# Six of a recurrent branch's eight output gates as seven-product pairs, computed behind the output projection

## The chip, the core and the metric

One core of a Trainium2 chip runs the whole layer. The metric is device time in microseconds (us); the time before is the median of three runs. TensorE multiplies, VectorE and ScalarE do elementwise work and empty TensorE's banks (PSUM), GpSimd (POOL) does elementwise work on SBUF, and SyncE (SP) issues the DMAs. In the profile PE is TensorE's matmul and PEld its weight load.

## The reference, cut to what matters

The layer is macaron FFN, mixer, macaron FFN, each modulated by a per-sample vector. In the mixer:

```
proj = h @ w_in
q, k, v, xr, yr, g_att, g_rec = jnp.split(proj, idx, axis=-1)
att = chunked_attention(q, k, v, rel_bias) @ w_att_o
xr = causal_depthwise_conv(xr, conv_w, conv_b)
rec = (rg_lru(xr, ...) * jax.nn.gelu(yr)) @ w_rec_o
merged = jax.nn.sigmoid(g_att) * att + jax.nn.sigmoid(g_rec) * rec
return merged @ w_out
```

Sequence, model width and recurrent width are 1024, all in float32. The stage of this case computes the gate g_rec and the projection by w_rec_o, and writes their product to DRAM (`part`), where a later stage fetches it.

## The kernel before, in words

A float32 matrix is cut into a high and a low part (`split`: ScalarE casts to the high part, VectorE or GpSimd subtracts for the low one), and one product of 128x128 weights with 512 columns takes three matmuls: high x high, high x low, low x high (`mm3`, L492 to L494). `proj` computes one block of 128 output channels: two halves of the sequence, eight chunks of depth, 48 matmuls.

The stage `rec_out_phase` has eight gate blocks ("gr", input `hh`, `hl`) and eight output blocks ("ro", input `rec_h`, `rec_l`), all by `proj`. They alternate: gate 0, gate 1, output 0, gate 2, output 1, and so on. ScalarE applies a tanh to a gate (L1289), VectorE multiplies it into the output (L1301), SP writes it to `part`. `Weights` loads weights two blocks ahead (`prep_cols`, `prep`); the float32 tile has the tag "raw" (three buffers), the parts "wh" and "wl" (four each).

Beside this runs `bg`: four modulation vectors, each of eight loads of 512 KB into the same "raw" buffers (`ada_acc`, SP), eight products on VectorE (L207, L209), and then eight narrow matmuls (`pc`, L223; the first two vectors) or four matmuls from a split accumulator (`pg`, L311 and L312; the two gates). A call `bg(4)` records four steps; it is called before and after each output block. Temporary tiles `tu` have three buffers, `t4` 22.

The scheduler of the language orders this stage: it places the recorded instructions of each engine in a fixed order, by its own rules. In a `tc.manual_schedule` region the engines named keep the order of the code; SP's DMAs are placed by the scheduler. Each engine executes its list from top to bottom. The FFN phases already use a seven-product scheme (`mix`, `product`, `block`): two products of halves of weights and input are combined so that seven of 12 matmuls replace eight, at the price of sums of weights and inputs.

Before this stage runs the recurrence (`lru_phase.rest`), behind it attention (`att_phase`), whose first matmuls (L1359) are the q and k projections.

Of the kernel before, what the change touches and what calls it, by code (L numbers as in the profile page):

```python
# [50 lines left out]
def kernel(  # L51
# [49 lines left out]
    def bank(name):  # L101
        return ps[0].tile([P, 512], F32, tag="ps", bufs=nbank[0], name=nm(name))
# [1003 lines left out]
    C_Q, C_K, C_V, C_XR, C_YR, C_GA, C_GR = 0, 512, 1024, 1536, 2560, 3584, 4608  # L1106
# [38 lines left out]
    def lru_phase(hh, hl, tail):  # L1145
# [125 lines left out]

        return SimpleNamespace(fetch=wts.fetch, head=head, rest=rest)

    def rec_specs():
        specs = {}
        for n in range(KB + 1):
            if n < KB:
                specs["gr", n] = partial(prep_cols, w_in, C_GR + n * P)
            if n > 0:
                specs["ro", n - 1] = partial(prep_cols, w_rec_o[0], (n - 1) * P)  # L1280
        for n in ("q", "k"):
            specs[n, 0] = partial(prep_cols, w_in, (C_Q if n == "q" else C_K))
        return specs

    def rec_out_phase(hh, hl, rec_h, rec_l, wts, part):
        def gate(n):
            tg = tu("tg")
            for sh, pj in enumerate(proj(wts["gr", n], hh, hl)):
                nc.scalar.activation(tg[:, sh * 512 : (sh + 1) * 512], pj, AF.Tanh, scale=0.5)  # L1289
            return tg  # L1290

        nxt = gate(0)
        for n in range(KB):
            tg = nxt
            if n + 1 < KB:
                nxt = gate(n + 1)
            bg(4)
            pr = proj(wts["ro", n], rec_h, rec_l)
            for sh in range(2):
                sl = slice(sh * 512, (sh + 1) * 512)  # L1300
                nc.vector.scalar_tensor_tensor(tg[:, sl], tg[:, sl], 1.0, pr[sh], op0=ALU.add, op1=ALU.mult)  # L1301
            nc.sync.dma_start(part[n * P : (n + 1) * P, :], tg)
            bg(4)
        bg_flush()

    def att_phase(hh, hl, wts0, tg_dram, n_ga):
        att_h, att_l = [], []
# [618 lines left out]
    with tc.tile_pool(name="psA", bufs=1, space=PSUM) as psA, tc.tile_pool(name="tmpA", bufs=1) as tmpA:  # L1926
        ps[0], tmp[0] = psA, tmpA
        with tc.manual_schedule(engines=ALL_ENGINES):
            hh, hl = new_h()
            f1 = ffn(0, ffn1_w_gu, ffn1_w_down, hh, hl, x, out if upto == 1 else x1)  # L1930
            startup(f1, hh, hl)
        bgq.extend([ada_gate(0, 0.5), ada_cols(3), ada_cols(4)])
        if upto == 1:
            f1.run(None, None, 3)
            return
        nxt = new_h()
        lru_run = lru_phase(*nxt, rec_specs())
# [6 lines left out]
        rec_out_phase(hh, hl, rec_h, rec_l, wts, part)  # L1944
    n_ga = sum(GATES)
    att_h, att_l = att_phase(hh, hl, wts, tg_dram, n_ga)
    with tc.tile_pool(name="psB", bufs=1, space=PSUM) as psB, tc.tile_pool(name="tmpC", bufs=1) as tmpC:
# [4 lines left out]
        nxt = new_h()  # L1952
# [45 lines left out]
```

## Time and profile before

| what | value |
|---|---|
| median of three runs | 2185.45 us (2184.38 to 2185.84) |
| the profiled execution's own time | 2184.91 us |
| its span | 2183.1 us |
| granted TensorE clock, mean | 0.997 |

How to read it: the page gives each engine's busy time; the time windows give it for stretches, with the granted clock and the DMA share; the groups join instructions of one line, operation and shape, with count, mean ns of one and the idle time ahead of them with what ended it; the timeline shows single instructions (start, duration, engine, line, out<-in, idle time before and who ended it). A matmul of TensorE is shown with its full length, and the next starts before it ends.

### The profile page before, as it was taken

Reading aid. Unit: us, or ns where it says so; the run is one execution under the profiler, and the core shown is the slowest. Engines: PE = TensorE matmul, PEld = TensorE weight load, DVE = VectorE, ACT = ScalarE, POOL = GpSimd, SP = SyncE. Lnnn points to the kernel's source line nnn. Section 1 sums busy time; section 2 is a strip of 40 time slices with the busy share of each in tenths; the row PEclk is TensorE's granted clock in tenths of the full one; section 3 lists DMA queues with packets and bytes.
Section 4 is the critical chain, followed back from the end, with each engine's and each line's share of the span. In section 5 each row is a group of like instructions: output and inputs, shape, how many; then the busy total and the mean of one; then the engine's idle time right before and its main releaser. Section 6 shows DMA issues by size and latency. Waiting matters only on the chain.

```text
span 2183.1 us, 26770 instructions
## 1 busy us (share of the span) xinstructions
PE 2142.9 (98%) x9973; PEld 1778.6 (81%) x9973; DVE 1311.2 (60%) x1699; ACT 1015.7 (47%) x1572; POOL 699.3 (32%) x514
## 2 busy tenths in 40 slices
PE   7999999999999999999999999999999999999998
PEld 5878788888878888888898988888888888888877
DVE  7676675567467777654236666555686564544466
ACT  5443333334447787611147777436443333334443
POOL 1468895421104011000121120002168883522102
PEclk9999999999999999999999999999999999999999
DMA  9357674468575111276311011464357663347365
GB/s 326 90 177 261 226 260 154 138 219 317 189 248 189 48 51 42 75 240 211 132 49 61 26 56 55 147 196 164 111 197 260 238 220 111 113 152 274 127 230 184
DMA packets 261498, 358.36 MB, mean 164 GB/s; under 512 B 16720, under 2 KB 170488, under 8 KB 261368
## 3 DMA queue, kind: packets, MB, share of 16 engines
q1 hardware_dynamic: 248448, 310.43, 43.0%
q10 hardware_dynamic: 12920, 46.23, 5.5%
q8 instruction: 78, 1.28, 0.2%
q14 instruction: 52, 0.43, 0.1%
HBM read 265.37 MB, written 94.37 MB: 165 GB/s over the span
## 4 chain that ended last, share of the span: by engine, by line
PE 79%; DVE 6%; ACT 4%; DMA 2%; issue 1%; POOL 1%; SPq 0%; POOLq 0%; DVEq 0%; ACTq 0%
PE px L1008 8%; PE pv L1008 7%; PE pj L494 6%; PE pj L492 6%; PE pj L493 6%; PE psX L747 6%; PE psX L748 6%; PE psX L749 6%; PE pj L1359 5%; PE psZ L747 3%; PE psZ L749 3%; PE psZ L748 3%; PE pv L1406 2%; DMA rawd<-downs 1%; PE psY L749 1%; PE psY L747 1%
## 5 line engine op out<-in xcount | busy, mean ns | idle before, releaser
L149 ACT CAST dh<-rawd 128x1024 fp32r<-128x1024 f32 x154 | 161.1, 1053 | 204.2 <-PE px L1008 60.1
L150 DVE TENSOR_TENSOR dh<-rawd,dh 128x1024 fp32r<-128x1024 f32 x130 | 162.3, 1253 | 153.2 <-ACT dh L149 148.6
L738 DVE TENSOR_TENSOR wm<-raw,wm 128x512 fp32r<-128x512 f32 x152 | 162.5, 1073 | 152.4 <-ACT wm L737 149.5
L492 PE MATMUL pj<-hh,wh 128*128 128x512 f32 x562 | 220.8, 393 | 0.0
L493 PE MATMUL pj<-hl,wh 128*128 128x512 f32 x562 | 219.2, 390 | 0.8 <-DVE hl L355 0.8
L494 PE MATMUL pj<-hh,wl 128*128 128x512 f32 x562 | 219.4, 390 | 0.3 <-DVE wl L150 0.2
L1008 PE MATMUL px<-dh,dh 128*128 128x512 f32 x608 | 187.5, 390 | 1.2 <-DVE dh L150 1.2
L344 POOL TENSOR_SCALAR rstd<-rstd 128x1 f32<-128x1 f32 x47 | 29.9, 636 | 424.4 <-ACT junk L343 423.0
L1008 PE MATMUL pv<-dh,dh 128*128 128x512 f32 x528 | 163.2, 391 | 2.4 <-DVE dh L150 2.4
L149 ACT CAST wh<-raw 128x1024 fp32r<-128x1024 f32 (+1 forms) x84 | 84.7, 1011 | 145.3 <-DMA raw<-in_w_in_dram 41.7
L150 POOL TENSOR_TENSOR wl<-raw,wh 128x1024 fp32r<-128x1024 f32 x20 | 48.3, 2421 | 294.6 <-ACT wh L149 249.9
L946 POOL TENSOR_TENSOR act<-act,act 128x512 f32<-128x512 f32 x54 | 87.2, 1614 | 160.7 <-DMA act<-act 115.9
L1008 PE MATMUL px<-dh 128*128 128x512 f32 x352 | 137.4, 390 | 0.0
L1008 PEld LDWEIGHTS px<-dh,dh 128*128 128x128 f32 x608 | 114.0, 188 | 25.4 <-DVE dh L150 2.0
L494 PEld LDWEIGHTS pj<-hh,wl 128*128 128x128 f32 x562 | 105.5, 188 | 22.9 <-DVE wl L150 1.2
L493 PEld LDWEIGHTS pj<-hl,wh 128*128 128x128 f32 x562 | 105.6, 188 | 22.8 <-DVE hl L355 1.4
L492 PEld LDWEIGHTS pj<-hh,wh 128*128 128x128 f32 x562 | 105.7, 188 | 21.3 <-DVE a L527 0.3
L150 DVE TENSOR_TENSOR wl<-raw,wh 128x1024 fp32r<-128x1024 f32 (+1 forms) x64 | 73.7, 1155 | 78.0 <-ACT wh L149 77.8
L1008 PEld LDWEIGHTS pv<-dh,dh 128*128 128x128 f32 x528 | 98.8, 188 | 24.4 <-DVE dh L150 4.1
L747 PE MATMUL psX<-hh,wm 128*128 128x512 f32 x296 | 115.6, 390 | 2.1 <-ACT mixes L770 2.1
L747 PE MATMUL psX<-hs,wm 128*128 128x512 f32 x296 | 115.8, 391 | 1.3 <-ACT mixes L763 1.1
L749 PE MATMUL psX<-hs,wm 128*128 128x512 f32 x296 | 115.3, 389 | 0.0
(335 smaller groups left out, 5717.8 us busy)
## 6 DMA issues: line engine op xcount, KB each, us to landing
rawa<-in_w_ada_dram SPq DMA_DIRECT2D x56, 512.0 KB, 4.7
raw<-in_ffn_w_gu_dram SPq DMA_DIRECT2D x47, 512.0 KB, 5.5
rawd<-acts SPq DMA_DIRECT2D x88, 256.0 KB, 3.8
rawd<-downs SPq DMA_DIRECT2D x88, 256.0 KB, 4.1
raw<-in_w_in_dram SPq DMA_DIRECT2D x44, 512.0 KB, 3.7
act<-act SPq DMA_DIRECT2D x37, 512.0 KB, 5.0
acts<-act ACTq DMA_DIRECT2D x36, 512.0 KB, 4.0
sr<-in_ffn_w_gu_dram SPq DMA_DIRECT2D x35, 512.0 KB, 6.0
```

The costliest lines, as they stand in the source:

```text
L149: nc.scalar.copy(hi, raw)
L150: (eng or nc.vector).tensor_tensor(lo, raw, hi.bitcast(F32), op=ALU.subtract)
L492: nc.tensor.matmul(dst, wh[:, kk, :], xhk[:, sl], start=first, stop=False)
L493: nc.tensor.matmul(dst, wh[:, kk, :], xlk[:, sl], start=False, stop=False)
L494: nc.tensor.matmul(dst, wl[:, kk, :], xhk[:, sl], start=False, stop=last)
L738: nc.vector.tensor_tensor(t[:, 1], src, t[:, 0].bitcast(F32), op=ALU.subtract)
L747: nc.tensor.matmul(dst, t[:, 0, kk, :], xh, start=first and kk == 0, stop=False, skip_group_check=True)
L748: nc.tensor.matmul(dst, t[:, 0, kk, :], xl, start=False, stop=False, skip_group_check=True)
L749: nc.tensor.matmul(dst, t[:, 1, kk, :], xh, start=False, stop=last and kk == 3, skip_group_check=True)
L946: nc.gpsimd.tensor_tensor(o, p, q, op=op)
L1008: nc.tensor.matmul(dst, a_[:, 0, tk], w_[:, 1, :], start=first and n == 0, stop=last and n == 2, skip_group_check=True,)
L1359: nc.tensor.matmul(d, a[:, k, :], b[k][:, sl], start=k == 0 and i == 0, stop=k == KB - 1 and i == 2)
```

## The change

Gate blocks 0 and 4 stay plain and come first. Then the eight output blocks follow each other, in the order 0, 4, 1, 5, 2, 6, 3, 7. For 0 and 4 gate and output are multiplied as before. The other six outputs are copied to SBUF by ScalarE (`pr`) and written to DRAM (`rec_raw`). `bg` is called with 8 steps before and 4 after each output block. The sums of the input that the pairs need are recorded here too, six of them (`sum_of`, `combine`: three operations on VectorE, a cast on ScalarE, a low part on VectorE).

Then, in the order of the code (`manual_schedule`), the gates (1, 5), (2, 6), (3, 7) are computed as pairs: the weights of the two blocks are mixed by VectorE (`mix`) to seven sets, each cut into parts; `product` does 12 matmuls of one set with halves or sums of the input. Products 1, 2, 5 and 3 run pair by pair, then 6 over the pairs, then 7, then 4. `chain[j]` is a bank (`grX`) into which products 1, 6, 7 and 4 of a pair add up, `b2` (`grY`) takes product 2, `b3` (`grZ`) products 5 and 3; copies and additions between them form the gates `T`. `close` fetches the raw output and multiplies. The weights of q and k are loaded from here (`qk_w`).

```diff
+    GR_PLAIN = (0, 4)
+    GR_PAIRS = ((1, 5), (2, 6), (3, 7))
+    RO_ORDER = (0, 4, 1, 5, 2, 6, 3, 7)
...
+        def combine(i, kk, plus, minus):
+            t = tv("hsum")
+            vec(t, *plus, ALU.add)
+            for m in minus:
+                vec(t, t, m)
+            hs[i, kk] = s = t4("hs", F32R, (P, 2, 512))
+            nc.scalar.copy(s[:, 0], t)
+            vec(s[:, 1], t, s[:, 0].bitcast(F32))
...
+        def mix(j, i):
+            g, u = raws[j]
+            a, b, c, e = g[:, :4], g[:, 4:], u[:, :4], u[:, 4:]
+            if i == 5:
+                vec(c, a, c)
+                vec(a, a, c)
+                vec(a, a, e, ALU.add)
+            if i == 3:
+                vec(a, e, c)
+                vec(b, b, a)
+            src = {1: a, 2: b, 5: a, 3: b, 6: a, 7: c, 4: e}[i]
...
+            nc.scalar.copy(t[:, 0], src)
+            vec(t[:, 1], src, t[:, 0].bitcast(F32))
...
-        nxt = gate(0)
-        for n in range(KB):
-            tg = nxt
-            if n + 1 < KB:
-                nxt = gate(n + 1)
-            bg(4)
+        tgs = {n: gate(n) for n in GR_PLAIN}
+        early_sums = [(5, kk) for kk in range(4)] + [(6, 0), (6, 1)]
+        for at, n in enumerate(RO_ORDER):
             pr = proj(wts["ro", n], rec_h, rec_l)
+            bg(8)
...
+                sum_of(*early_sums[at - 2])
             bg(4)
         bg_flush()
...
+            for j, (n, m) in enumerate(GR_PAIRS):
+                T[n], T[m] = t4("tg"), t4("tg")
+                chain[j], b2 = bank("grX"), trbank("grY")
+                product(j, 1, chain[j], True)
+                nc.scalar.copy(T[n][:, h1], chain[j])
+                if j < 2:
+                    mix(j + 1, 1)
+                product(j, 2, b2, True)
+                vec(T[n][:, h1], T[n][:, h1], b2, ALU.add)
+                nc.scalar.activation(T[n][:, h1], T[n][:, h1], AF.Tanh, scale=0.5)
+                if j < 2:
+                    mix(j + 1, 2)
+                    some(1)
+                else:
+                    mix(0, 6)
+                b3[j] = bank("grZ")
+                product(j, 5, b3[j], True)
+                nc.scalar.copy(T[m][:, h2], b3[j])
...
+                product(j, 3, b3[j], False)
...
+            for j, (n, m) in enumerate(GR_PAIRS):
+                product(j, 6, chain[j], False)
+                nc.scalar.copy(T[n][:, h2], chain[j])
+                vec(T[n][:, h2], T[n][:, h2], b3[j], ALU.add)
+                nc.scalar.activation(T[n][:, h2], T[n][:, h2], AF.Tanh, scale=0.5)
+                mix(j, 7)
+                some(1)
...
+            for j, (n, m) in enumerate(GR_PAIRS):
+                product(j, 4, chain[j], False)
+                close(n)
+                nc.scalar.activation(T[m][:, h1], chain[j], AF.Tanh, scale=0.5)
```

What becomes of the order. First TensorE at the first modulation vector. Before, the column matmuls `pc` of its accumulator stand between a gate block (`pj_7290`, input `hh`) and an output block (`pj_7361`, input `rh`):

```order
L493 MATMUL pj_7290<-hl_958,wh_7143 128x512
L494 MATMUL pj_7290<-hh_950,wl_7144 128x512
L223 MATMUL pc_7342<-ones_r,acc_7199 128x1 x8
L492 MATMUL pj_7361<-rh_5918,wh_7213 128x512
L493 MATMUL pj_7361<-rl_5919,wh_7213 128x512
```

After, they stand inside the second output block (`pj_7303`, `pj_7304`, block 4), behind 15 of its 48 matmuls:

```order
L493 MATMUL pj_7303<-rl_6289,wh_7144 128x512
L494 MATMUL pj_7303<-rh_6288,wl_7145 128x512
L223 MATMUL pc_7284<-ones_r,acc_7256 128x1 x8
L492 MATMUL pj_7304<-rh_6288,wh_7144 128x512
L493 MATMUL pj_7304<-rl_6289,wh_7144 128x512
```

They moved forward by 33 matmuls of this block and by the gate block that stood ahead of them.

Second, the fourth vector. ScalarE casts the two halves of its accumulator (`acch`), TensorE multiplies them (`pg`). Before, on ScalarE, the last output weights (`wh_8019`, `wh_8077`) stand ahead of the second half's cast:

```order
L149 CAST acch_7937<-acc_7791 128x512
L149 CAST wh_7943<-raw_7941 128x1024
L149 CAST wh_8019<-raw_8017 128x1024
L149 CAST wh_8077<-raw_8075 128x1024
L149 CAST acch_8004<-acc_7791 128x512
```

After, the weights of the last two output blocks (`wh_7622`, `wh_7689`) stand behind both casts and behind a copy of an earlier output (`pr_7676`):

```order
L149 CAST acch_7589<-acc_7505 128x512
L149 CAST acch_7608<-acc_7505 128x512
L1393 COPY pr_7676<-pj_7626 128x512
L149 CAST wh_7622<-raw_7620 128x1024
L1393 COPY pr_7676<-pj_7627 128x512
L149 CAST wh_7689<-raw_7687 128x1024
```

What moved is the weight of the seventh output block, from ahead of the vector's second half to behind it.

Third, ScalarE in the pair stage, which has no counterpart before: there it held for each gate two tanh, beside casts of weights and of the vectors' halves:

```order
L1289 ACTIVATE tg_7716<-pj_7724 128x512
L149 CAST wh_7871<-raw_7869 128x1024
L1289 ACTIVATE tg_7868<-pj_7875 128x512
L1289 ACTIVATE tg_7868<-pj_7876 128x512
L149 CAST acch_7937<-acc_7791 128x512
```

After, for the second pair (`tg_8002`, `tg_8003`; `wm` are parts of mixed weights, `hs` parts of input sums), between the copies of `grX` and `grZ`:

```order
L1417 COPY tg_8002<-grX_8004 128x512
L1361 CAST wm_8019<-raw_7903 128x512
L1422 ACTIVATE tg_8002<-tg_8002 128x512
L1361 CAST wm_8036<-raw_7903 128x512
L1307 CAST hs_8043<-hsum_8039 128x512
L1430 COPY tg_8003<-grZ_8046 128x512
L1361 CAST wm_8063<-raw_7903 128x512
```

The copy of `grZ`, on which product 3 of this pair waits, is behind the cast of an input sum and behind the tanh. VectorE's list between the same two points:

```order
L1294 TENSOR_TENSOR tg_8002<-tg_8002,grY_8005 128x512
L1294 TENSOR_TENSOR wm_8036<-raw_7903,wm_8036 128x512
L1294 TENSOR_TENSOR hsum_8039<-hh_948,hl_956 128x512
L1294 TENSOR_TENSOR hsum_8039<-hsum_8039,hh_944 128x512
L1294 TENSOR_TENSOR hsum_8039<-hsum_8039,hl_952 128x512
L1294 TENSOR_TENSOR hs_8043<-hsum_8039,hs_8043 128x512
L1294 TENSOR_TENSOR sr_7904<-raw_7903,sr_7904 128x512
```

Each `wm` and `hs` row subtracts a part that ScalarE's row of the same name has just cast. L1294 is `vec`, the helper of all these operations.

More of the change, by code (lines that the diff above doesn't have):

```diff
@@ L1283, in rec_specs, with vec, f32 @@
         return specs
     def rec_out_phase(hh, hl, rec_h, rec_l, wts, part):
+        h1, h2 = slice(0, 512), slice(512, 1024)
+        rec_raw = dpool.tile([D, S], F32, name="rec_raw")
+        qk_w = Weights({
+            (n, 0): partial(prep_cols, w_in, (C_Q if n == "q" else C_K)) for n in ("q", "k")
+        })
+        def vec(out, p, q, op=ALU.subtract):
+            nc.vector.tensor_tensor(out, p, q, op=op)
+        def f32(t, sl):
+            return t[:, sl].bitcast(F32)
+        hs = {}
@@ new lines, in combine, with both, halves @@
+        def combine(i, kk, plus, minus):
[6 more added lines that the diff above has]
+            vec(s[:, 1], t, s[:, 0].bitcast(F32))
+        def both(k, sl):
+            return f32(hh[k], sl), f32(hl[k], sl)
+        def halves(i, kk):
+            t = hs[i, kk]
+            return t[:, 0].bitcast(F32), t[:, 1].bitcast(F32)
@@ new lines, in rec_out_phase, with load @@
+        raws, mixed = {}, {}
+        def load(j):
+            n, m = GR_PAIRS[j]
+            g = wpool.tile([P, KB, P], F32, tag="raw", bufs=3, name=nm("raw"))
+            u = t4("sr", F32, (P, KB, P))
+            for t, c in ((g, n), (u, m)):
+                c0 = C_GR + c * P
+                nc.sync.dma_start(t, w_in[:, c0 : c0 + P].rearrange("(k p) n -> p k n", p=P))
+            raws[j] = g, u
+        turn = [0]
+        def mix(j, i):
+            g, u = raws[j]
+            a, b, c, e = g[:, :4], g[:, 4:], u[:, :4], u[:, 4:]
+            if i == 5:
+                vec(c, a, c)
[5 more added lines that the diff above has]
+            src = {1: a, 2: b, 5: a, 3: b, 6: a, 7: c, 4: e}[i]
+            tag = ("wh", "wl")[turn[0] % 2]
+            turn[0] += 1
+            t = wpool.tile([P, 2, 4, P], F32R, tag=tag, bufs=4, name=nm("wm"))
+            nc.scalar.copy(t[:, 0], src)
+            vec(t[:, 1], src, t[:, 0].bitcast(F32))
+            mixed[j, i] = t
@@ L1286, in gate, with product @@
+        def product(j, i, dst, first):
+            t = mixed.pop((j, i))
+            for kk in range(4):
+                xh, xl = moving(i, kk)
+                nc.tensor.matmul(dst, t[:, 0, kk, :], xh, start=first and kk == 0, stop=False, skip_group_check=True)
+                nc.tensor.matmul(dst, t[:, 0, kk, :], xl, start=False, stop=False, skip_group_check=True)
+                nc.tensor.matmul(dst, t[:, 1, kk, :], xh, start=False, stop=kk == 3, skip_group_check=True)
         def gate(n):
@@ new lines, in rec_out_phase @@
+        early_sums = [(5, kk) for kk in range(4)] + [(6, 0), (6, 1)]
+        for at, n in enumerate(RO_ORDER):
+            pr = proj(wts["ro", n], rec_h, rec_l)
+            bg(8)
+            if n in tgs:
+                tg = tgs.pop(n)
+                for sh in range(2):
+                    sl = slice(sh * 512, (sh + 1) * 512)
+                    nc.vector.scalar_tensor_tensor(tg[:, sl], tg[:, sl], 1.0, pr[sh], op0=ALU.add, op1=ALU.mult)
+                nc.sync.dma_start(part[n * P : (n + 1) * P, :], tg)
+            else:
+                t = tu("pr")
+                for sh in range(2):
+                    nc.scalar.copy(t[:, sh * 512 : (sh + 1) * 512], pr[sh])
+                nc.sync.dma_start(rec_raw[n * P : (n + 1) * P, :], t)
+                sum_of(*early_sums[at - 2])
@@ L1303, in rec_out_phase, with some, close @@
             bg(4)
         bg_flush()
+        with tc.manual_schedule(engines=CORE_ENGINES):
+            T, chain, b3, late = {}, {}, {}, {}
+            load(0)
+            for i in (1, 2, 5, 3):
+                mix(0, i)
+            load(1)
+            load(2)
+            todo = [(6, 2), (6, 3)] + [(7, kk) for kk in range(4)]
+            def some(n):
+                for _ in range(n):
+                    if todo:
+                        sum_of(*todo.pop(0))
+            for j, (n, m) in enumerate(GR_PAIRS):
[11 more added lines that the diff above has]
+                    some(1)
+                else:
+                    mix(0, 6)
+                b3[j] = bank("grZ")
+                product(j, 5, b3[j], True)
+                nc.scalar.copy(T[m][:, h2], b3[j])
+                if j < 2:
+                    mix(j + 1, 5)
+                    some(1)
+                else:
+                    mix(1, 6)
+                    todo += [(4, kk) for kk in range(4)]
+                product(j, 3, b3[j], False)
+                if j < 2:
+                    mix(j + 1, 3)
+                    some(1)
+                else:
+                    mix(2, 6)
+                    some(1)
+            for j, (n, m) in enumerate(GR_PAIRS):
[4 more added lines that the diff above has]
+                mix(j, 7)
+                some(1)
+            for j, (n, m) in enumerate(GR_PAIRS):
+                product(j, 7, chain[j], False)
+                vec(T[m][:, h2], T[m][:, h2], chain[j], ALU.add)
+                nc.scalar.activation(T[m][:, h2], T[m][:, h2], AF.Tanh, scale=0.5)
+                mix(j, 4)
+                if j == 0:
+                    some(4)
+            def close(n):
+                pr = tu("pr")
+                nc.sync.dma_start(pr, rec_raw[n * P : (n + 1) * P, :])
+                nc.vector.scalar_tensor_tensor(T[n], T[n], 1.0, pr, op0=ALU.add, op1=ALU.mult)
+                nc.sync.dma_start(part[n * P : (n + 1) * P, :], T[n])
+            for j, (n, m) in enumerate(GR_PAIRS):
+                product(j, 4, chain[j], False)
+                close(n)
+                nc.scalar.activation(T[m][:, h1], chain[j], AF.Tanh, scale=0.5)
+                if j == 0:
+                    qk_w.fetch(2)
+                close(m)
@@ L1306, in att_phase @@
+        return qk_w
     def att_phase(hh, hl, wts0, tg_dram, n_ga):
@@ L1943 @@
         bgq.extend([ada_cols(6), ada_cols(7), ada_gate(1, 1.0), ada_gate(2, 0.5)])
-        rec_out_phase(hh, hl, rec_h, rec_l, wts, part)
+        wts = rec_out_phase(hh, hl, rec_h, rec_l, wts, part)
     n_ga = sum(GATES)
```

28 lines of the change are left out of this document (17 added, 11 removed).

## The prediction

> **What bounds the kernel now.** I read the page's busy table first, then the time windows over the stage that is changed, then its groups by line and shape, then the timeline of single engines. Times are us from the span's start.
>
> ```profile
> span 2183.1 us, 26770 instructions
> PE 2142.9 (98%) x9973; PEld 1778.6 (81%) x9973; DVE 1311.2 (60%) x1699; ACT 1015.7 (47%) x1572; POOL 699.3 (32%) x514
> ```
> ```profile
> 896.10:1077.00 180.90, 180.05 (x810) 148.91 (x808) 89.82 (x88) 42.31 (x51) 4.79 (x2) 1.00 0.54 180
> ```
>
> The second fence is a window over the stage (columns: length, then busy us of PE, PEld, DVE, ACT, POOL, granted clock, DMA share, GB/s). TensorE is busy for 180.05 of 180.90 us at clock 1.00: here time is the number of matmuls. VectorE is half idle and POOL almost empty. So fewer matmuls save time only while the others still keep up.
>
> ```profile
> L492 PE MATMUL pj<-hh,wh x128: 388/389/487, 896.1 to 1053.5; 128*128 128x512 f32 x128
> L492 PE MATMUL pj<-rh,wh x128: 388/389/487, 917.8 to 1075.3; 128*128 128x512 f32 x128
> ```
> ```profile
> 1054.64 0.39 PE L494 MATMUL pj<-rh,wl 128*128 128x512 f32 x1
> ...
> 1075.72 0.39 PE L494 MATMUL pj<-rh,wl 128*128 128x512 f32 x1
> 1076.96 0.51 PE L1359 MATMUL pj<-hh,wh 128*128 128x512 f32 x1 [0.85 <-DVE tg L1301]
> ```
>
> The gates begin at 896.1 and the first recurrent output block at 917.8. Between the two L494 matmuls lie 93 starts: 21.08/93 = 0.2267 us each. The 0.39 is a matmul's length, not its pitch. A block of 48 is 10.88 us, a product of 12 is 2.72 us. Attention starts at 1076.96.
>
> **The change, part by part.** The gain: a pair needs 7 x 12 = 84 matmuls for 96, three pairs 36 fewer: 36 x 0.2267 = **-8.2 us**. What it costs is on VectorE and ScalarE, priced by rows of this stage, where POOL is idle:
>
> ```profile
> L209 DVE SCALAR_TENSOR_TENSOR acc<-rawa,c_act,acc 128x1024 f32<-128x1024 f32 x28 | 35.9, 1284 | 10.6 <-DMA rawa<-in_w_ada_dram 10.3
> L150 DVE TENSOR_TENSOR wl<-raw,wh 128x1024 fp32r<-128x1024 f32 x14 | 17.2, 1226 | 32.1 <-ACT wh L149 32.1
> L150 DVE TENSOR_TENSOR acch<-acc,acch 128x512 fp32r<-128x512 f32 x4 | 2.8, 688 | 1.4 <-ACT acch L149 1.4
> L149 ACT CAST acch<-acc 128x512 fp32r<-128x512 f32 x4 | 2.5, 620 | 12.8 <-PE pg L311 7.4 <-DVE acc L209 5.4
> L1289 ACT ACTIVATE tg<-pj 128x512 f32<-128x512 f32 x16 | 9.1, 595 | 26.2 <-PE pj L494 24.9 <-DVE acch L150 0.9 <-DMA part<-tg 0.2
> L207 DVE TENSOR_SCALAR acc<-rawa,c_act 128x1024 f32<-128x1024 f32 x4 | 3.0, 750 | 0.0
> ```
>
> ```profile
> 940.00:960.00 20.00, 20.00 (x95) 16.79 (x96) 10.84 (x12) 3.08 (x4) 0.00 (x0) 1.00 0.69 226
> ```
>
> A 128x512 operation is 0.69 on VectorE, 0.6 on ScalarE; a modulation product over 1024 columns is 1.28 (the first of a vector 0.75).
>
> *The eight output blocks.* They now follow each other without gate blocks between, and four modulation vectors (32 loads, bg) are pressed into them at 12 steps a block, not 8 in two blocks. The rows of before that carry this: when VectorE's last recurrence step ended and the first vector's eighth product began, how long a load takes to land, how fast four loads followed each other, and what the column matmuls cost.
>
> ```profile
> 919.95 1.22 DVE L1226 TENSOR_TENSOR rl<-a,rh 128x1024 fp32r<-128x1024 f32 x1 [1.17 <-ACT rh L1225]
> ...
> 936.52 1.28 DVE L209 SCALAR_TENSOR_TENSOR acc<-rawa,c_act,acc 128x1024 f32<-128x1024 f32 x1 [0.79 <-DMA rawa<-in_w_ada_dram]
> ```
> ```profile
> rawa<-in_w_ada_dram SPq DMA_DIRECT2D x32, 512.0 KB, 4.1
> ```
> ```profile
> 924.51 7.46 SPq L204 DMA_DIRECT2D rawa<-in_w_ada_dram  x4
> ```
> ```profile
> 939.76 1.68 PE pc L223 x16
> ```
>
> The first vector is complete at 937.8; its column matmuls (pc, 1.68) ran at 939.76, behind a gate block. Now they stand 15 matmuls into the second output block: 917.8 + 10.88 + 3.4 = 932.1. VectorE starts on the vector about 1.05 later than at 921.1 (a weight cast now precedes the last square root), and has 0.75 + 7 x 1.28, six sums and two gate products of 0.69 to do: 922.2 + 15.2 = 937.4. TensorE waits **5.3**. Before the second vector stand 8 products (9.7), a weight's low part (1.2), nine sums (6.2), two gate products (1.4) and the wait for pc: done at about 957.1, when TensorE arrives at 955.9: **1.2**. From there loads set the pace. Three "raw" buffers hold modulation rows and output weights alike; a turn of one is 4.1 landing, 1.28 product and about 1 of issue and waiting, so one load per 2.1 to 2.2 (four in a row took 7.46, three intervals of 2.4, with a weight's split among them). Eighteen more loads bring the fourth vector to 957.1 + 39 = 996. The gate matmuls (pg) on it stand ahead of the seventh block, and on ScalarE that block's weight cast stands behind their second operand and a copy, which itself waits for VectorE's low part of that operand. After 996: 0.6 + 0.7 + matmul 0.4 + cast 0.6 + low 1.4 (a gate addition is ahead) + copy 0.6 + cast 1.05, about 6: block seven starts at about 1002. TensorE, by its own count (955.9 + 1.2 + 1.7 + 1.6, three blocks, 1.8 for pg), is there at 994.8: **7**. Sum 13.5; the walk is loose by some us, I take **+13**. Bounds: with no DMA wait, VectorE has 38.8 us of products, 18 sums and four gate products (15.2), three low parts of weights (3.7) and about 4.5 of small work before the fourth vector is complete, 62 us from 922.2: it ends at 984.4, and only the first two waits and a little remain, +8; with a load every 2.4, +20.
>
> That a blocked cast holds what is behind it has a row in before:
>
> ```profile
> 1044.55 0.37 SPq L154 DMA_DIRECT2D raw<-in_w_in_dram  x1
> ```
> ```profile
> 1053.76 0.60 ACT L1289 ACTIVATE tg<-pj 128x512 f32<-128x512 f32 x1 [9.98 <-PE pj L494]
> 1054.25 1.04 ACT L149 CAST wh<-raw 128x1024 fp32r<-128x1024 f32 x1
> ```
>
> The weight was asked for at 1044.55, yet its cast ran only after the gate's tanh had waited 9.98 for TensorE.
>
> *The three pairs.* One row of before shows the detour that counts here, a low part on VectorE that waits for its cast (idle 0.69 in the brackets):
>
> ```profile
> 992.84 0.69 DVE L150 TENSOR_TENSOR acch<-acc,acch 128x512 fp32r<-128x512 f32 x1 [0.69 <-ACT acch L149]
> ```
>
> TensorE needs 252 x 0.2267 = 57.1. VectorE has 76 operations of 0.69, 52, but in series: every low part waits for a cast of the sum made just before it. Count zero at the first product. Product 1 and 2 end at 5.4; the addition to the gate starts at 5.7. From one pair's addition to the next pair's stand 21 VectorE operations (the addition, three low parts of weights, three sums of four each, five mixings of weights: 14.5) and five detours over ScalarE (0.69 each as in this row, one with a tanh ahead 1.2), 18.5 to 19 us; the first round has one low part more, 19.5. TensorE's part of it is four products, 10.9. Product 3 goes to the bank of product 5, whose copy on ScalarE stands behind the cast of a sum: it starts 5.9 after each addition. So additions at 5.7, 25.2, 44. For the last pair no sum stands there: its product 3 starts at 46.8 (addition 0.7, tanh 0.6, cast 0.6, copy 0.6, and handovers), the three products 6 run from 49.5 to 57.7. From 52.2, the end of the first of them, each pair costs copy, addition, tanh, cast, low part, three sum operations, cast, low part: 6.5 less overlaps, 6.1; three: 70.6. Addition, tanh, cast, low part, 2.6: product 4 at about 73.2, three of 2.72: 81.4. So **+24.3** over 57.1. Bounds: 0.62 a VectorE operation and 0.6 a detour give 17 a round, about 74: +17; a round of 21 gives +29.
>
> *What else moves.* Six raw outputs go to DRAM and back, 6.3 MB; DMA share is 0.54 and the pair stage loads little. The writes wait on SP in order behind modulation loads; without that cover a read would add some 4 at the end. The bias load for attention now stands behind the six closing writes, by my count 13 us into attention; the 96 matmuls ahead of the scores cover 22. Attention's first bank waits for the last tanh (0.6 and handovers) as it waited 0.85 for a product: nothing.
>
> Sum: -8.2 + 13 + 24.3 = **+29**. The profiled execution took 2184.91 (0.5 under the median 2185.45): 2214.
>
> **The rivals.** *Faster:* VectorE and ScalarE run so far ahead that TensorE never waits: 2184.91 - 8.2 = 2176.7. For it: 52 < 57, and VectorE busy 89.82 of 180.90. It decides if a pair's round falls under 10.9; the 14.5 of VectorE work alone is over that. 5%. *Only the output blocks wait*, the pairs hide: -8.2 + 13, 2189.7. 6%. *Only the pairs wait*, loads being faster than in before: 2201. 11%. *The clock falls too*, as it does in a stretch near the start of before (time windows, then TensorE's timeline):
>
> ```profile
> 14.00:16.00 2.00, 1.05 (x8) 0.70 (x7) 1.66 (x4) 0.58 (x1) 0.00 (x0) 1.00 1.20 292
> 16.00:18.00 2.00, 0.69 (x5) 0.61 (x5) 1.72 (x6) 1.72 (x4) 0.00 (x0) 0.85 1.17 305
> 18.00:20.00 2.00, 2.00 (x6) 1.52 (x6) 1.04 (x2) 2.00 (x4) 0.00 (x0) 0.50 1.10 348
> 22.00:24.00 2.00, 2.00 (x10) 1.66 (x9) 1.13 (x2) 1.25 (x2) 0.00 (x0) 1.00 1.11 337
> ```
> ```profile
> 17.66 0.80 PE L613 MATMUL pj<-hh,wh 128*128 128x512 f32 x1 [1.31 <-ACT hh L362]
> 18.25 0.63 PE L613 MATMUL pj<-hh,wl 128*128 128x512 f32 x1
> 18.68 0.63 PE L613 MATMUL pj<-hh,wh 128*128 128x512 f32 x1
> ```
>
> After four microseconds half idle the granted clock was 0.50 and matmuls started 0.43 apart: some eight of them, 8 x 0.2 = 1.6 us per fall. The pair stage has five or six such idle stretches. On its path lie those before the last products and product 3's: up to 8 us, 2222. 16%.
>
> The Trainium skill (TensorE: Matmul & The Clock Gate, HAM oscillation) asks for an idle gap of over about 3.4 us before the clock halves. By it only the gaps before product 3 would count, with VectorE's round behind them as cover, and the 16% of this case would go to the forecast's 2214. The row disagrees: the longest gap ahead of its fall was 1.31.
>
> **How the numbers follow.** The forecast has 62%. From no change a measurement of this kernel can tell about 0.2%, 4.4 us. Slower: forecast, pairs only, clock, half of the blocks-only case, 92%; same: its other half, 3%; faster 5%. The low bounds +8 and +17 with the gain give 2202, the pairs-only case 2201; the high bounds +20 and +29 give 2226, with the clock's 2222 inside. Range 2200 to 2226; it leaves out the first two rivals.
>
> **What would show it.** Right: VectorE near 0.65 busy and TensorE near 0.7 over the 80 us before attention; product 3 (grZ) waiting on ScalarE's copy 3 to 10 us; a wait of about 5 on pc and one before the seventh output block. Wrong: a pair stage of 60 us, pc not waiting, or attention starting before 1077.

## The result, and the profile after

The changed kernel took 2224.61 us (median of four runs, 2220.89 to 2225.44) against 2184.91 for the kernel before, measured beside it: a ratio of 1.0171, 95% interval 1.0158 to 1.0185. (This is the ratio recorded over the fast runs; the quotient of the two medians is 1.0182, inside the interval.) It is slower by 39.7 us. The forecast was 2214.0, 29 us slower, with a range of 2200 to 2226. The sign and the range held, and so did the mechanism of the pair stage; the term of the output blocks was much too small.

The page of the profiled execution (2225.44 us), then TensorE's waits between 880 and 1125 us (total, times, longest):

```profile
span 2223.6 us, 26865 instructions
PE 2154.0 (97%) x9937; PEld 1780.5 (80%) x9937; DVE 1379.9 (62%) x1796; ACT 1042.3 (47%) x1624; POOL 697.6 (31%) x514
```
```profile
PE grZ L1369 <- ACT tg L1430: 12.8, 3, 7.2
PE grX L1369 <- ACT wm L1361: 5.6, 3, 2.6
PE pc L223 <- DVE acc L209: 4.8, 2, 4.3
PE pg L311 <- ACT acch L149: 4.2, 2, 3.2
PE pj L492 <- ACT wh L149: 0.8, 1, 0.8
PE pj L1527 <- ACT tg L1468: 0.7, 1, 0.7
PE pg L312 <- DVE acch L150: 0.6, 1, 0.6
```

TensorE has 36 matmuls less and yet is busy 11 us longer (2154.0 for 2142.9). Before, it had one wait of 0.85 in this stretch; now it has 29.5 us of them. Both facts have the same root, as its timeline shows (start, duration, and in the brackets the idle time ahead):

```profile
936.50 3.57 PE L223 MATMUL pc<-ones_r,acc 128*128 128x1 f32 x16 [4.28 <-DVE acc L209]
...
960.20 1.95 PE L223 MATMUL pc<-ones_r,acc 128*128 128x1 f32 x16 [0.57 <-DVE acc L209]
...
1003.68 0.80 PE L311 MATMUL pg<-acch,ones_r 128*128 128x512 f32 x1 [3.19 <-ACT acch L149]
...
1032.71 0.39 PE L1369 MATMUL grX<-hh,wm 128*128 128x512 f32 x1
...
1064.17 0.79 PE L1369 MATMUL grZ<-hh,wm 128*128 128x512 f32 x1 [7.21 <-ACT tg L1430]
...
1105.87 0.67 PE L1369 MATMUL grX<-hs,wm 128*128 128x512 f32 x1 [2.61 <-ACT wm L1361]
...
1116.59 0.50 PE L1527 MATMUL pj<-hh,wh 128*128 128x512 f32 x1 [0.69 <-ACT tg L1468]
```

Look at the durations behind the waits: 0.79 and 0.80, where the first matmul behind a wait otherwise takes 0.50 (as at 1116.59), and 3.57 for the sixteen narrow ones. The same sixteen in the timeline of before, where no wait stands ahead of them:

```profile
939.60 1.84 PE L223 MATMUL pc<-ones_r,acc 128*128 128x1 f32 x16
```

That is the clock. (In TensorE's list the column matmuls of the first vector moved forward by 33 matmuls in all: 192 of this stage stood ahead of them, now 159.) The time windows behind the first, the second and the last of the vectors' waits, and over the pair stage (length, busy us of PE, PEld, DVE, ACT, POOL, granted clock, DMA share, GB/s):

```profile
936.00:946.00 10.00, 9.50 (x31) 8.21 (x32) 6.94 (x11) 1.67 (x2) 0.00 (x0) 0.52 0.75 248
946.00:951.00 5.00, 5.00 (x24) 4.12 (x23) 2.19 (x3) 0.00 (x0) 0.00 (x0) 1.00 0.70 218
962.00:966.00 4.00, 4.00 (x13) 3.14 (x13) 3.81 (x7) 2.22 (x4) 0.00 (x0) 0.58 0.73 230
1004.00:1013.00 9.00, 7.62 (x15) 4.66 (x15) 7.00 (x9) 5.70 (x9) 0.00 (x0) 0.50 1.03 339
1032.70:1116.60 83.90, 64.86 (x254) 50.12 (x252) 56.47 (x83) 31.36 (x54) 1.76 (x1) 0.92 0.15 50
```

Now the account. From attention's start before (1076.96) to after (1116.59) it is 39.6, which is the whole difference. The pairs' first product starts at 1032.71; with no wait it would be at 896.1 + 480 x 0.2267 + 3.4 (two pc) + 1.8 (pg) = 1010.1. So the **output blocks cost 22.6**: waits of 4.28 + 0.57 + 1.02 + 3.19 + 0.61 + 0.77 = 10.4, and the clock, estimated as busy time by its missing share, 9.50 x 0.48 + 4.00 x 0.42 + 7.62 x 0.50 = 10.0; some 2 are left over. The **pair stage** lasts 83.9 for 57.1 of products, **+26.8**. With -8.2 for the matmuls this is 41.2; the kernel before had 1.6 of such losses itself (180.90 less 768 x 0.2267 and 5.2).

VectorE in the first round of the pairs, from one addition to the next:

```profile
1038.35 0.69 DVE L1294 TENSOR_TENSOR tg<-tg,grY 128x512 f32<-128x512 f32 x1 [0.89 <-PE grY L1371]
1040.25 0.69 DVE L1294 TENSOR_TENSOR wm<-raw,wm 128x512 fp32r<-128x512 f32 x1 [1.21 <-ACT wm L1361]
1040.86 0.69 DVE L1294 TENSOR_TENSOR hsum<-hh,hl 128x512 f32<-128x512 f32 x1
1041.58 1.42 DVE L1294 TENSOR_TENSOR hsum<-hsum,hs 128x512 f32<-128x512 f32 x2
1043.68 0.69 DVE L1294 TENSOR_TENSOR hs<-hsum,hs 128x512 fp32r<-128x512 f32 x1 [0.68 <-ACT hs L1307]
...
1058.35 0.68 DVE L1294 TENSOR_TENSOR tg<-tg,grY 128x512 f32<-128x512 f32 x1
```

The round is 20.0 us: operation behind operation, and before each low part (`wm`, `hs`) an idle gap in which ScalarE casts.

### The profile page after: what moved, and what is told of

Same layout as the page of the kernel before. It is cut to its first block, busy times and chain, and to the rows that moved or that the text cites. A ratio compares the mean times of both kernels' runs of the same rounds, so it can differ in the third digit from the quotient of the medians.

```text
span 2223.6 us, 26865 instructions
## 1 busy us (share of the span) xinstructions
PE 2154.0 (97%) x9937; PEld 1780.5 (80%) x9937; DVE 1379.9 (62%) x1796; ACT 1042.3 (47%) x1624; POOL 697.6 (31%) x514
## 4 chain that ended last, share of the span: by engine, by line
PE 73%; DVE 10%; ACT 7%; DMA 5%; issue 3%; POOL 2%; SPq 0%; POOLq 0%; DVEq 0%; ACTq 0%
PE px L1008 8%; PE pv L1008 7%; PE psX L747 5%; PE psX L749 5%; PE psX L748 5%; PE pj L1527 5%; PE pj L492 4%; PE pj L494 4%; PE pj L493 4%; PE psZ L747 3%; PE psZ L749 3%; PE psZ L748 3%; DMA rawd<-downs 2%; PE pv L1574 1%; PE psY L749 1%
## 5 line engine op out<-in xcount | busy, mean ns | idle before, releaser
L492 PE MATMUL pj<-hh,wh 128*128 128x512 f32 x466 | 183.2, 393 | 0.0
L493 PE MATMUL pj<-hl,wh 128*128 128x512 f32 x466 | 181.7, 390 | 0.8 <-DVE hl L355 0.8
L494 PE MATMUL pj<-hh,wl 128*128 128x512 f32 x466 | 181.9, 390 | 0.3 <-DVE wl L150 0.2
L1008 PEld LDWEIGHTS px<-dh,dh 128*128 128x128 f32 x608 | 113.9, 188 | 25.2 <-DVE dh L150 1.7
L747 PE MATMUL psX<-hh,wm 128*128 128x512 f32 x296 | 115.7, 391 | 2.3 <-ACT mixes L770 2.3
L747 PE MATMUL psX<-hs,wm 128*128 128x512 f32 x296 | 115.8, 391 | 1.3 <-ACT mixes L763 1.2
L748 PE MATMUL psX<-hs,wm 128*128 128x512 f32 x296 | 115.2, 389 | 0.0
L749 PE MATMUL psX<-hs,wm 128*128 128x512 f32 x296 | 115.2, 389 | 0.0
L749 PE MATMUL psX<-hh,wm 128*128 128x512 f32 x296 | 115.2, 389 | 0.0
L748 PE MATMUL psX<-hl,wm 128*128 128x512 f32 x296 | 115.2, 389 | 0.0
L737 ACT CAST wm<-raw 128x512 fp32r<-128x512 f32 x152 | 92.6, 613 | 45.8 <-POOL raw L725 45.7
L149 ACT CAST wh<-raw 128x1024 fp32r<-128x1024 f32 (+1 forms) x78 | 78.2, 1007 | 65.5 <-PE po L1818 23.1
```

The source lines that it names most:

```text
L149: nc.scalar.copy(hi, raw)
L492: nc.tensor.matmul(dst, wh[:, kk, :], xhk[:, sl], start=first, stop=False)
L493: nc.tensor.matmul(dst, wh[:, kk, :], xlk[:, sl], start=False, stop=False)
L494: nc.tensor.matmul(dst, wl[:, kk, :], xhk[:, sl], start=False, stop=last)
L737: nc.scalar.copy(t[:, 0], src)
L747: nc.tensor.matmul(dst, t[:, 0, kk, :], xh, start=first and kk == 0, stop=False, skip_group_check=True)
```

## The experiments

The stage in all kernels, from the timelines (us; "pair stage" is from the pairs' first product to attention's first matmul, "attention" that matmul's start; before: 1076.96). Ratios are to the kernel before. The medians are of several executions, the other columns of one. Where the output blocks are those of the kernel after, the stretch from their first matmul to the pairs' start still takes 111.5 to 117.3 in these single executions, so the pair edits are judged by the pair stage, not by the total.

| kernel | median | ratio, 95% interval | pairs' start | pair stage | attention |
|---|---|---|---|---|---|
| after | 2224.61 | 1.0171 [1.0158, 1.0185] | 1032.7 | 83.9 | 1116.6 |
| output blocks alone | 2206.47 | 1.0095 [1.0078, 1.0111] | | | 1099.2 |
| 6 steps a block | 2211.55 | 1.0123 [1.0107, 1.0140] | 1013.5 | 89.9 | 1103.3 |
| covered column matmuls | 2226.34 | 1.0179 [1.0162, 1.0196] | 1034.0 | 83.8 | 1117.8 |
| copy earlier | 2226.58 | 1.0192 [1.0173, 1.0211] | 1033.8 | 87.7 | 1121.4 |
| sums on GpSimd | 2213.96 | 1.0127 [1.0109, 1.0146] | 1036.0 | 69.4 | 1105.4 |
| low parts later | 2215.37 | 1.0137 [1.0121, 1.0154] | 1028.3 | 77.0 | 1105.3 |
| three pair edits | 2220.69 | 1.0160 [1.0144, 1.0175] | 1031.2 | 80.4 | 1111.6 |
| three edits, 7 steps | 2210.19 | 1.0107 [1.0090, 1.0124] | 1022.5 | 80.7 | 1103.2 |
| low parts later, 6 steps | 2197.54 | 1.0052 [1.0038, 1.0066] | 1015.4 | 72.9 | 1088.2 |
| two pairs, two plain | 2190.58 | 1.0023 [1.0014, 1.0032] | 1014.3 | 68.9 | 1083.2 |

### The output blocks

**Alone.** The pair stage is replaced by plain gates:

```diff
-            for j, (n, m) in enumerate(GR_PAIRS):
...
+        for n in RO_ORDER[2:]:
+            tg = gate(n)
+            pr = tu("pr")
+            nc.sync.dma_start(pr, rec_raw[n * P : (n + 1) * P, :])
+            nc.vector.scalar_tensor_tensor(tg, tg, 1.0, pr, op0=ALU.add, op1=ALU.mult)
```

> The output blocks as in the kernel after (order, modulation steps, raw outputs to DRAM, six input sums, which nothing reads here), then the six gates as plain blocks, no pairs. It measures the output blocks' term by itself. Theory: 22 us over the kernel before, as the trace of the kernel after has it from the first output block to the first pair product: 2204 to 2209. Rival: the forecast's 13 was right for the blocks, and the pairs reach back into them: 2196 to 2200.

Measured: 2206.47, 21.6 over before. So the two stages add (the other 18.1 of the total are about the pairs' 26.8 less the 8.2 of the matmuls), and the blocks' term is 22, not the forecast's 13: the theory held, the rival fell. TensorE's waits sum to 10.3 here (pc 4.5, pg 3.4, a weight 1.0, a tanh 1.4), so half of the 21.6 is not in the waits themselves.

**6 steps a block.**

```diff
-            bg(8)
+            bg(3)
...
-            bg(4)
+            bg(3)
```

> The four modulation vectors are taken through the output blocks at 6 steps a block in place of 12 (3 before, 3 after); the rest is the kernel after. The column matmuls then stand at the start of the third and of the fifth output block, the last gate matmuls at the start of the pairs. Theory: the waits of some 10 us in the output blocks go, and the clock with them stays at 1.00 there: 18 to 22 us less, 2203 to 2207, the pair stage as before. Rival: the clock falls there whatever TensorE waits for (the narrow matmuls, or VectorE's load): only the waits go, 2213 to 2216. Second rival: the vectors now end so late that the pairs wait for them instead: 2218 to 2225.

Measured: 2211.55, 13 less than after and between the ranges that were expected. The output blocks did what the theory said: the pairs start at 1013.5, 19.2 earlier, with the clock back but for one dip (below, in the last section):

```profile
940.11 1.95 PE L223 MATMUL pc<-ones_r,acc 128*128 128x1 f32 x16
...
1013.46 0.50 PE L1369 MATMUL grX<-hh,wm 128*128 128x512 f32 x1
```
```profile
940.00:1013.00 73.00, 72.30 (x325) 59.67 (x326) 46.55 (x51) 13.11 (x21) 0.00 (x0) 0.98 0.87 287
```

No wait stands at the column matmuls any more, and TensorE is busy for 72.30 of 73.00 us. But 6 us of it are given back: the pair stage is 89.9 instead of 83.9, because the fourth vector's last halves now fall into the first pair (its gate matmuls run at 1012.8 to 1018.5, between those of product 1, and VectorE's work for them stands among its mixing: the first addition starts 11.8 after the first product, where it was 5.6). The theory had the gain of the blocks right and missed what it cost the pairs, which is what the second rival named: about a third of the gain.

**Is it the wait that takes the clock?** The kernel after, with TensorE kept busy ahead of the first vector's column matmuls by 36 matmuls whose result is overwritten:

```diff
         pc = trbank("pc")
+        if v == 6:
+            for _ in range(36):
+                nc.tensor.matmul(pc, ones_r, hh[0][:, 0:512], start=True, stop=True)
```

> The kernel after, with 36 matmuls of 512 columns, whose result is overwritten, ahead of the first vector's column matmuls, in the same bank. All of it now stands right behind the first output block, so that TensorE is busy from about 929 to 937 while it would wait; 15 real matmuls come later than they did. Theory: the wait is what lowers the clock; it then stays at 1.00 over 929 to 951, but for 3 to 4 us behind the narrow matmuls as in the run with 6 steps; some 4 to 6 us of clock and slow narrow matmuls come back, 3.4 go to the 15 matmuls: 2220 to 2225 in all. Rival: the clock falls there without the wait, for the narrow matmuls or what else runs: half clock from 936 to 945 as before, 2226 to 2231.

Measured: 2226.34. The total lies in the rival's range. But in the profiled execution the gates themselves began 4.4 later than in the kernel after, for something ahead of the stage that I did not follow, so the total decides nothing (counted from the gates, the pairs start 3.1 earlier); the rows do. First the timeline, then the windows:

```profile
933.05 8.32 PE L224 MATMUL pc<-hh,ones_r 128*128 128x512 f32 x36
...
960.75 3.57 PE L226 MATMUL pc<-ones_r,acc 128*128 128x1 f32 x16 [4.53 <-DVE acc L209]
```
```profile
929.00:952.00 23.00, 22.91 (x110) 18.96 (x109) 21.17 (x27) 2.93 (x4) 0.00 (x0) 1.00 0.80 271
960.00:970.00 10.00, 9.25 (x30) 7.99 (x31) 5.96 (x9) 1.05 (x1) 0.00 (x0) 0.50 0.78 248
```

With the wait covered, the clock is 1.00 over the stretch in which it had been 0.52, though the same narrow matmuls run in it (1.95 at 941.45) and VectorE is no less busy. The wait has moved to the second vector (4.53), and there the clock goes to 0.50 for 10 us. These two waits, of 4.3 and 4.5 us, cost twice: themselves, and about as much again in half clock behind them.

### The pairs

**The copy earlier.** Product 5 and the copy of its bank ahead of the mixing and the sum:

```diff
+                b3[j] = bank("grZ")
+                product(j, 5, b3[j], True)
+                nc.scalar.copy(T[m][:, h2], b3[j])
                 if j < 2:
                     mix(j + 1, 2)
                     some(1)
-                b3[j] = bank("grZ")
-                product(j, 5, b3[j], True)
-                nc.scalar.copy(T[m][:, h2], b3[j])
```

> In the pair loop product 5 and the copy of its bank grZ now stand ahead of the next pair's mixing for product 2 and the input sum. Theory: VectorE's serial round of some 20 us sets the pace of the pair stage, and the place of the copy only moves idle time inside a round; additions to the gates stay 19 to 20 us apart, gain 0 to 3 us: 2221 to 2225. Rival: the copy of grZ behind the casts sets the pace, since the three waits for it cost TensorE 12.8 us; they go, and with them 10 to 13 us: 2211 to 2215.

Measured: 2226.58, no gain, and a little above the theory's 2221 to 2225. The additions on VectorE stand no closer than in the kernel after (20.0 and 19.0), 22.0 and 19.5:

```profile
1039.40 0.69 DVE L1294 TENSOR_TENSOR tg<-tg,grY 128x512 f32<-128x512 f32 x1 [0.89 <-PE grY L1371]
1061.36 0.68 DVE L1294 TENSOR_TENSOR tg<-tg,grY 128x512 f32<-128x512 f32 x1
1080.88 0.68 DVE L1294 TENSOR_TENSOR tg<-tg,grY 128x512 f32<-128x512 f32 x1
```

The largest wait in the list of the kernel after, 12.8 us for the copy of grZ, is a symptom. Here it grew to 16.9: the copy still stands behind the tanh, the tanh behind the addition, and the addition behind VectorE's round. The rival fell. (The copy ahead of the tanh as well was run only together with other edits, further down.)

**The sums on GpSimd,** the ten that are made in the pair stage:

```diff
-            vec(t, *plus, ALU.add)
+            eng = nc.gpsimd if raws else None
+            vec(t, *plus, ALU.add, eng)
             for m in minus:
-                vec(t, t, m)
+                vec(t, t, m, eng=eng)
```

> The additions and subtractions of the ten input sums made in the pair stage (30 operations) run on GpSimd instead of VectorE; casts and low parts stay. Theory: VectorE's round loses 6 or 9 operations of 0.69 and a detour or two, some 6 us in each of two rounds, and the chain ahead of the last products loses some: 14 to 18 us, 2207 to 2211. Rival: GpSimd at 1.6 us an operation, 48 us in all, delivers late and ScalarE's casts stand waiting for it, ahead of copies and tanh: no gain or slower, 2222 to 2230. Second rival: TensorE's own handovers (copy, tanh, bank) set the pace: 2222 to 2225.

Measured: 2213.96, 10.6 less; the pair stage is 69.4 instead of 83.9 (the pairs start 3.3 later here). Taking work from VectorE shortens the stage, by 14.5, within the 14 to 18 that the theory gave, and neither rival fits. The total is above the expected 2207 to 2211 because the pairs started later. The rounds, though, are 15.7 and 16.7, where 14 had been expected (20 less 6). VectorE's own operations got longer. First a group of VectorE in the pair stage of the kernel after, then the same group with the sums on GpSimd (busy, mean ns):

```profile
L1294 DVE TENSOR_TENSOR raw<-raw,sr 128x512 f32<-128x512 f32 x4 | 2.8, 692 | 0.1
```
```profile
L1294 DVE TENSOR_TENSOR raw<-raw,sr 128x512 f32<-128x512 f32 x4 | 6.6, 1659 | 0.1
```

In that kernel's timelines, VectorE, then GpSimd:

```profile
1050.48 0.68 DVE L1294 TENSOR_TENSOR hs<-hsum,hs 128x512 fp32r<-128x512 f32 x1
...
1051.80 1.66 DVE L1294 TENSOR_TENSOR raw<-raw 128x512 f32<-128x512 f32 x1
```
```profile
1048.39 1.63 POOL L1294 TENSOR_TENSOR hsum<-hsum,hl 128x512 f32<-128x512 f32 x1
1051.24 1.67 POOL L1294 TENSOR_TENSOR hsum<-hh,hl 128x512 f32<-128x512 f32 x1 [1.23 <-DVE hs L1294]
```

At 1050.48 GpSimd rests and VectorE takes 0.68; at 1051.80 GpSimd runs and the same amount of work takes 1.66, as long as one of GpSimd's. The Trainium skill (SBUF — State Buffer, SBUF: two separate sides) says that an operation of VectorE with two SBUF inputs and one of GpSimd that reads SBUF take a shared pair of ports in turns, each for its whole length. The rows agree: GpSimd's operation ends at 1052.91, and VectorE's, begun under it, 0.55 later, somewhat less than the 0.68 that one takes alone.

**The low parts later.** Each low part is recorded one group of work later, so that VectorE has something to do while ScalarE casts (`lows` makes those that are pending):

```diff
             nc.scalar.copy(t[:, 0], src)
-            vec(t[:, 1], src, t[:, 0].bitcast(F32))
+            lows()
+            pend["mix", j, i] = t[:, 1], src, t[:, 0].bitcast(F32)
```

> In the pair stage every low part (of a mixed weight or an input sum) is put one group of VectorE's work later, so that it stands behind other work while ScalarE casts. Nothing else changes. Theory: VectorE's round loses its detours of 0.69, some 3.5 us in each of two rounds, and one or two more where a mixed weight is waited for ahead of the last products: 5 to 9 us less than the kernel after, 2216 to 2220. Rival: the detours are not what makes the round, since ScalarE is late with the casts anyway: 2223 to 2226.

Measured: 2215.37, 9.2 less. The pair stage is 77.0, so 6.9 less, and the theory held for it; the pairs also started 4.4 earlier here, which this edit does not touch. The additions are 14.7 and 14.5 apart, and VectorE is busy for 14.2 and 13.5 of these: hardly a gap is left. Some seven us of the gain were lost by the edit itself:

```profile
1100.49 0.79 PE L1383 MATMUL grX<-hs,wm 128*128 128x512 f32 x1 [7.00 <-DVE wm L1294]
```
```profile
1094.20 5.63 DVE L1474 SCALAR_TENSOR_TENSOR tg<-tg,pr 128x1024 f32<-128x1024 f32 x3
1099.76 0.68 DVE L1294 TENSOR_TENSOR wm<-sr,wm 128x512 fp32r<-128x512 f32 x1
```

The last low part came to stand behind the closing products (`close`, L1474), which wait for reads from DRAM.

**All three pair edits at once**, with product 5 ahead of the addition too:

```diff
+                b3[j] = bank("grZ")
+                product(j, 5, b3[j], True)
+                nc.scalar.copy(T[m][:, h2], b3[j])
                 vec(T[n][:, h1], T[n][:, h1], b2, ALU.add)
```

> Pair stage only: the sums on GpSimd, the low parts one group later, and product 5 with the copy of its bank ahead of the addition and the tanh. Theory: VectorE's round falls to 12 operations of 0.69 and one or two detours, 9 to 10 us, under TensorE's 10.9; TensorE's waits for grZ go but for about one handover each: 7 to 11 us under the kernel with the sums on GpSimd alone, 2203 to 2207. Rival: the bank's own copy and ScalarE's order hold TensorE as before: 2210 to 2214.

Measured: 2220.69, outside what either theory gave, and worse than two of its parts alone. Seven us are the same lost low part. For the rest, the additions are 17.5 and 15.7 apart, longer than with all sums left on VectorE (14.7 and 14.5). In the second round VectorE idles for 1.6 only, yet its twelve operations take 14.1, which would be 8.3 at 0.69 each: GpSimd adds with few pauses now (13.22 of 15.70; the columns are those of the windows above), and nearly each operation of VectorE meets one of its own. That the gaps closed by the later low parts were those in which GpSimd had worked undisturbed is my reading of it, not shown apart. Some 4 us more behind the rounds I did not follow.

```profile
1054.42:1070.12 15.70, 11.18 (x47) 8.29 (x45) 14.09 (x13) 4.46 (x9) 13.22 (x9) 0.98 0.00 1
```

**The same with the vectors at 7 steps a block** (`bg(4)` before, `bg(3)` after):

> The pair stage as in the kernel with all three edits, and the modulation vectors at 7 steps an output block (4 before, 3 after), so that the last gate matmuls stand inside the last output block. Theory: the two terms add up: the output blocks lose 18 to 20 of their 22 us, the pairs 18 to 22 of theirs: 2184 to 2190, no faster than before beyond what can be told. Rival: all waits gone, 2177 to 2180. Second rival: the loads of the vectors run into the pairs' weights and hold VectorE there: 2192 to 2198.

Measured: 2210.19, above all that was expected. The pair stage is as bad as in the run before (80.7), and at 7 steps the third vector's gate matmuls were placed ahead of their operand: one wait of 9.71 at 986. The start of the pairs is 1022.5, between the two other paces.

**What worked, together:** sums on VectorE, low parts one group later, the last one ahead of the closing, 6 steps a block.

```diff
+            lows()
             def close(n):
```

> All sums stay on VectorE. Low parts one group later as before, but the last mixed weight's low part now stands ahead of the closing products, which wait for reads from DRAM (in the run before it stood behind them, and the last product waited 7.00 for it); and the modulation vectors at 6 steps an output block. Theory: the two gains add but for what the vectors' ends cost inside the first pair (some 6 in the run with 6 steps): pair start at 1013.5, pair stage 70 plus 3 to 6, attention at 1087 to 1090, total 2195 to 2199. Rival: the closing was no real loss, since the other products would wait for VectorE there: 2202 to 2206.

Measured: 2197.54, attention at 1088.2, as the theory said. Of the kernel after's 39.7 us of loss, 27 are gone, and it is still slower than before.

**Cover for VectorE.** Two pairs only; gates 1 and 5 are plain blocks, one behind each pair's four products. Product 5 and its copy stand ahead of the addition, and the mixing for products 6, 7 and 4 is recorded earlier than before; the rest is as in the kernel just above. The diff is cut:

```diff
-    GR_PAIRS = ((1, 5), (2, 6), (3, 7))
+    GR_PAIRS = ((2, 6), (3, 7))
+    GR_COVER = (1, 5)
...
                 product(j, 3, b3[j], False)
+                pjs = proj(cover.pop(c), hh, hl)
```

> As the run with both, but gates 1 and 5 are plain blocks again (24 matmuls less than before the change, not 36), one after each pair's products 1, 2, 5 and 3, as work for TensorE while VectorE mixes and sums; product 5 and its bank's copy ahead of the addition. Theory: a round of TensorE is now 21.8 us, over VectorE's 19, so that the pairs hardly wait: -5.4 for the matmuls, +3.4 for the output blocks, +2 to 5 for the start and the tail: 2184 to 2188, no different from before. Rival: VectorE's start, with the vectors' ends and the first pair's mixing, holds TensorE: 2190 to 2196. Second rival: nothing waits, and the clock stays at 1.00: 2179 to 2182.

Measured: 2190.58, ratio 1.0023 [1.0014, 1.0032]: above the expected 2184 to 2188, at the lower edge of the first rival, and slower than the 2185.88 of before beside it by 4.7, little but clear of the noise. The waits of TensorE from 880 to 1125 are down to 8.7 us, none over 1.8, about half of them where the first rival has them (the vectors' ends and the start of the first pair, 988 to 1019), and the clock stays at 1.00:

```profile
940.00:1011.00 71.00, 69.50 (x319) 56.86 (x318) 45.27 (x50) 12.78 (x20) 0.00 (x0) 1.00 0.84 279
1011.00:1083.00 72.00, 65.02 (x277) 50.98 (x275) 57.10 (x82) 30.18 (x50) 0.28 (x1) 1.00 0.41 129
```

What remains is small and spread: 24 matmuls less are worth 5.4, and 8.7 of waits eat them. With a start 0.7 later this gives about half of the 6.2 by which attention starts later than before; the other half I did not follow. No version that I tried beats the kernel before.

## Why the prediction was right or wrong

- **The pair stage, +24.3: right, +26.8 measured.** The walk held almost row for row, counted from the first product at 1032.71: additions at 5.6, 25.6 and 44.7 (5.7, 25.2, 44), the third products at 11.5, 31.5 and 47.1 (11.6, 31.1, 46.8), product 4 at 73.2 (73.2), the end at 83.9 (81.4). The cause, VectorE's serial round with detours over ScalarE, is shown: 20.0 became 14.7 without the detours, while an earlier copy gained nothing. The 2.5 that are missing are in the last three products at a lower clock and the wait of 0.69 for the last tanh.
- **The output blocks, +13: this step failed, +22.6 measured,** outside its own bounds of +8 to +20. The waits as such were put too high, not too low: 13.5 forecast, 10.4 of idle time measured (pc 4.28 for 5.3, the second pc 0.57 for 1.2, at block seven 4.6 for 7, and 1.0 at the third vector). What the step left out is the clock, about 10 us. Part of that sits inside the forecast's 7: block seven starts 6.9 behind TensorE's own count, since the gate matmuls on the way to it run at half clock. I had seen the clock fall behind a wait in the trace of before, and priced it for the pairs alone.
- **"One load per 2.1 to 2.2": too fast.** The second vector was complete at 960.2 for 957.1, the fourth at 1002.9 for 996. Between them lie the forecast's eighteen loads, sixteen of the vectors and two of weights, in 42.8 us: 2.4 each, the rate of its high bound. Block seven waited no longer than forecast all the same, because the waits and the slower clock had made TensorE 6.4 later than its count as well.
- **"The clock falls too", 16%, up to 8 us in the pair stage: right on the kind, wrong on the place.** There it costs about 2, since the falls at product 3 lie under VectorE's round; in the output blocks, where nothing covers them, 10. The price of 1.6 us per fall, from the first microseconds of before, was too low: the three falls in the output blocks cost 4.6, 1.7 and 3.8.
- **The rule of the Trainium skill** that I weighed (TensorE: Matmul & The Clock Gate, HAM oscillation: idle gaps of over about 3.4 us) fits the falls behind 4.28, 4.53 and 7.21, and nearly those behind 3.15 and 3.19. By it, the forecast's own waits of 5.3 and 7 in the output blocks should have been followed by half clock; I applied it to the pairs alone. It does not cover the fall behind 2.61 at 1105.87, nor that at 962 to 966, ahead of which the idle time was 0.57 and then sixteen narrow matmuls ran.
- **The matmuls, -8.2, and the other rivals.** That TensorE would not wait, or only in one stage, has fallen with the waits above; the output blocks alone (2206.47) and the pairs' 26.8 show both terms by themselves.
- **"What would show it":** over the 80 us before attention VectorE is busy 0.70 (0.65 forecast) and TensorE 0.76 (0.7); product 3 waits for the copy of grZ 2.4 to 7.2 (3 to 10); pc waits 4.28 (about 5).

That the range held was partly luck. The measured 2224.61 is 1.4 under its upper end. The output blocks missed by +9.6 (the clock +10, the waits -3, some 2 left over) and the pairs by +2.5, and 1.6 came back that the kernel before lost itself; the high bound had room for this only because it took both stages at their worst, and the clock was inside it only as a rival for another stage.

## What to carry to other kernels

Fewer matmuls are worth something only where the other engines' serial path per product stays under TensorE's; count operations and cast detours from row to row, and look for work with no such path to put between. When an edit makes TensorE wait for several microseconds on its own path, price the wait twice: the idle time, and the half clock behind it, which here cost 1.7 to 4.6 us a fall, unless another engine's longer round covers it. The largest wait in a list may be a symptom: follow it back to the engine that is never idle for long, and change that.

## What the runs showed of the hardware

- The granted clock was about half behind every wait of 3.15 us and more in the kernel after and in the run with the cover. It stayed there for 9 to 10 us behind the waits of 4.28 and 4.53 (0.52 over 936 to 946, 0.50 over 960 to 970), in which the narrow matmuls ran first; from the first 512-column matmul on it was 5.7 and 6.1. Behind the longest wait, 7.21 ahead of product 3, it was 4.4. Of two waits alike, one of 2.63 left the clock at 1.00 and the next, of 2.61, did not (0.53 over 1105.8 to 1109.4). The rows for 7.21 and 2.63:

```profile
1064.10:1068.40 4.30, 4.23 (x10) 3.36 (x11) 3.49 (x6) 0.63 (x2) 0.00 (x0) 0.50 0.00 0
1099.90:1102.90 3.00, 2.96 (x12) 2.10 (x12) 2.68 (x4) 0.20 (x1) 0.00 (x0) 1.00 0.00 0
```

  A run of sixteen narrow matmuls (128x1) behind a wait of 0.57 was followed by 4 us at 0.58. Without a wait the same narrow matmuls left it at 1.00 in the run with the cover and in the run with two pairs, but in the run with 6 steps it was at about 0.57 from 942 to 946:

```profile
942.00:944.00 2.00, 2.00 (x7) 1.57 (x7) 1.80 (x3) 0.14 (x1) 0.00 (x0) 0.58 1.08 349
944.00:946.00 2.00, 2.00 (x7) 1.58 (x6) 1.91 (x3) 1.95 (x3) 0.00 (x0) 0.56 0.75 234
```

  What decides between these cases stays open.
- VectorE's 128x512 operation on two SBUF inputs takes 1.66 instead of 0.69 where GpSimd works on SBUF meanwhile (mean of the group shown above), so that 30 operations moved to GpSimd (20.7 us of VectorE) left VectorE only 8.2 less busy in the pair stage (48.30 here, 56.47 in the kernel after):

```profile
1036.00:1105.00 69.00, 61.21 (x253) 48.20 (x251) 48.30 (x52) 30.04 (x54) 36.63 (x25) 0.95 0.17 53
```
